# Output projection of a hybrid attention and HGRN2 layer: the order of its token tiles written out by hand, and its norms moved between ScalarE, VectorE and GpSimd

## The chip, the cores and the metric

The kernel runs on one core of one Trainium2 chip. The metric is the device time of one execution in microseconds (us). The core has a matrix engine (TensorE, PE in the rows), VectorE (DVE), ScalarE (ACT), GpSimd (POOL) and SyncE (SP), which in this kernel issues all the loads and stores. TensorE's weight loads are shown as PEld; they overlap its products.

## The reference

One layer over 2048 tokens of width 1024. A combined projection feeds two parallel groups of heads: differential attention (4 heads of width 128) and a bidirectional HGRN2 scan (4 heads of width 128). Each head's readout is normalised by its own root mean square, multiplied by a gate, and all 8 heads go through one output projection. The stage that changes computes this (lines cut to what matters):

```python
def _rms_norm(x, g):
    xf = x.astype(jnp.float32)
    return xf * lax.rsqrt(jnp.mean(xf * xf, axis=-1, keepdims=True) + EPS) * g.astype(jnp.float32)
def _merge(attn_o, ag, hgrn_o, hg, w_out):
    y = jnp.concatenate([attn_o * jax.nn.silu(ag), hgrn_o * jax.nn.silu(hg)], axis=-1)
    return y @ w_out
...
        y_lat = _merge(attn_lat, ag_l, hgrn_lat, hg_l, w_out[layer])
...
        x = _layer_norm(alpha * x + gate[:, None, :] * y_lat, ln_gain[layer], ln_bias[layer])
```

Everything is float32. The kernel writes each float32 factor of a product as a high part in a rounded form (F32R) and a remainder in the same form, so that one product becomes three: lo by hi, hi by lo, hi by hi.

## The kernel before, in words

The kernel has three stages: the projections with the scan beside them, the attention, and the output projection (class `Output`). The last one, from about 1820 us, is what changes. It works on 16 tiles of 128 tokens, t = 0 to 15. The weight of 1024 by 1024 stays in SBUF: its first 512 columns as `woh` and `wol`, the other 512 in slots that attention has left, so that they carry old names (`kh`, `kl`, `e`).

For each tile there is a **front** and a **back**.

- `front(t)` loads the gates `G` and the readouts `Od` of the tile (512 KB each). ScalarE squares the 8 heads in one instruction of 128x1024, VectorE sums each head's squares (TENSOR_REDUCE), ScalarE takes the root, VectorE its reciprocal `rs`, and GpSimd multiplies the readouts by it (L1269). TensorE turns the 8 heads (8 transposes of 128x128 into PSUM, two banks of four, `pt`). For each bank VectorE multiplies by the gate (L1278) and rounds to the high part (a cast, L1279), and GpSimd subtracts to get the low part (L1280). The two parts are the stationary operands of the tile's products.
- `back(t)` loads the tile's rows of `x`, runs 24 products for each half of the columns (8 row blocks by three products, 128x512 each, into a PSUM bank `py`), and after each half VectorE multiplies by `gate` (L1304), adds ALPHA times `x` (L1305) and takes statistics (L1307). Behind the second half comes the LayerNorm's end: VectorE aggregates, ScalarE takes a root, VectorE a reciprocal and the product `nb` (L1327), ScalarE applies both to the row block (L1328), VectorE multiplies by `lng` (L1329), GpSimd adds `lnb` (L1330), SyncE stores.

Even tiles keep their readouts and gated parts in slots named `kh` and `kl`, odd ones in slots named `e`; tiles 0 and 1 use `q` and `e` for `x` and `y` and their fronts and most products run inside attention. In `run` the programme writes for each tile the five first steps of the front two tiles ahead, then the back's first half, then what is left of the next tile's front. A scheduler orders the engines' queues in this stage, by its own estimate of times; it may put the loads much earlier, and it put the first loads of `x` for tiles 2 and 3 at about 1215 us. Inside attention the order of TensorE, ScalarE and VectorE is written by hand. Every engine, SyncE too, works through its own queue in order; an instruction that waits for another engine holds all that stand behind it.

The last tile has its columns cut in four parts of 256, and its end on VectorE in two halves.

Of the kernel before, what the change touches and what calls it, by code (L numbers as in the profile page):

```python
# [22 lines left out]
F32, F32R, U32 = dt.float32, dt.float32r, dt.uint32  # L23
AF = mybir.ActivationFunctionType
ALU = mybir.AluOpType
# [4 lines left out]
P = 128  # L30
D = 1024
KT = 8
# [3 lines left out]
NKT = KEYS // P  # L36
H = 4
BLK = 512
NBLK = SEQ // BLK
GRID_W = 64  # L40
ALPHA = 2.0 ** 0.25
EPS = 1e-5
LAMBDA_INIT = 0.2
UW = 256
# [74 lines left out]
class Build:  # L119
    def __init__(self, nc, tc, I, out):  # L120
        self.nc, self.tc, self.I, self.out = nc, tc, I, out
# [9 lines left out]
    def run(self):  # L131
        nc, tc = self.nc, self.tc
        pool = tc.tile_pool
        with pool(name="dram", bufs=1, space=DRAM) as self.dram, \
                pool(name="const", bufs=1) as self.const:
            self.dram_tiles()
            att, output = Attention(self), Output(self)
            with ExitStack() as keys, ExitStack() as proj, ExitStack() as out:
                held = self.phase_project(att, proj, keys)
                att.run(held, proj, keys, output, out)  # L140
                output.run(out)
# [670 lines left out]
NT = SEQ // P  # L812
# [16 lines left out]
class Attention:  # L829
# [18 lines left out]
    def open(self, keys):  # L848

        self.kv0 = self.b.pool(keys, "kv0", 1, side="right")  # L850
        self.kv1 = self.b.pool(keys, "kv1", 1, side="right")
# [272 lines left out]
class Output:  # L1124
    def __init__(self, b):
        self.b, self.nc = b, b.nc
        self.gated = {}

    def open(self, stack):
        self.wo = self.b.pool(stack, "wo", 1)  # L1130
# [88 lines left out]
    def run(self, out):  # L1219
        b = self.b  # L1220
        self.op = b.pool(out, "o", 2)
        self.xy = lambda t: [self.op.tile([P, D], F32, name=nm) for nm in "xy"]
        self.py = b.pool(out, "py", 4, space=PSUM)
        self.acc = lambda n: self.py.tile([P, BLK], F32, name="py")
        pt = b.pool(out, "pt3", 2, space=PSUM)
        self.bank = lambda: pt.tile([P, 4, P], F32, name="pt3")
        for nm in ("lng", "lnb"):
            self.broadcast(nm, b.I[nm].unsqueeze(0), out)
        for t in range(2):
            for _ in self.backs[t]:  # L1230
                pass
        for t in range(2, NT):
            for _ in range(5 if t + 2 < NT else 0):
                self.advance(t + 2)
            for n in self.back(t):
                if n == 1 and t + 1 < NT:
                    while self.advance(t + 1):
                        pass

    def advance(self, t):  # L1240

# [106 lines left out]
```

## Time and profile before

| | |
|---|---|
| median of three runs | 2031.61 us (2031.46 to 2032.01) |
| the profiled execution's own time | 2032.69 us |
| its span from the first to the last instruction | 2030.9 us, so 1.8 us lie around it |
| TensorE busy, whole span | 1913.6 us (94%) |
| VectorE, GpSimd, ScalarE busy | 71%, 47%, 45% |
| mean granted TensorE clock | 0.981 of full speed |

The chain that ended last is TensorE for 66% of the span and VectorE for 14%. In the output projection (about 1820 us to the end) each full tile takes TensorE some 12 us of work; the stretch is read by tiles below. A row of a timeline gives the start, the duration, the engine, the line, the operation with its operands and shapes and, in brackets, how long the engine had been idle and which engine's work ended that.

### The profile page before, as it was taken

The numbers are of one execution on the slowest core, as the hardware profiler recorded it, in microseconds if no ns is written. First come the engines' busy times: TensorE is split into PE (matmuls) and PEld (weight loads), VectorE is DVE, ScalarE is ACT, GpSimd is POOL, SyncE is SP. The second block draws the span as 40 slices with busy tenths as digits, with TensorE's granted clock in tenths as the row PEclk, the third lists the DMA queues.
The fourth block names the chain that finished last, engine by engine and source line by source line (L and its number), as shares of the span: only waits on it lengthen the run. The fifth ranks groups of instructions, "written<-read, shape, count | busy, mean of one in ns | idle before, by whom it ended". The sixth has DMA issues, their size and how long they took to land.

```text
span 2030.9 us, 32106 instructions
## 1 busy us (share of the span) xinstructions
PE 1913.6 (94%) x11716; PEld 1693.3 (83%) x11716; DVE 1438.3 (71%) x3022; ACT 920.4 (45%) x1383; POOL 955.6 (47%) x697
## 2 busy tenths in 40 slices
PE   5899999999989999999879999999999999998887
PEld 3689888998878898877667999999999999887676
DVE  8940475455676755678454279999999999967878
ACT  6731233222222222232100168999998889852211
POOL 6400063343554532535110047877877767755543
PEclk8999999999989999999889999999999999999999
DMA  5772564523344543353657652261261031145442
GB/s 221 248 221 81 186 220 164 182 99 125 113 136 150 167 151 138 110 169 102 199 169 229 199 148 59 68 169 54 62 169 57 28 102 37 51 136 173 154 139 92
DMA packets 177760, 278.05 MB, mean 137 GB/s; under 512 B 16577, under 2 KB 108993, under 8 KB 175554
## 3 DMA queue, kind: packets, MB, share of 16 engines
q1 hardware_dynamic: 177602, 276.00, 42.6%
q8 instruction: 93, 1.52, 0.3%
q14 instruction: 65, 0.53, 0.1%
HBM read 178.94 MB, written 97.00 MB: 136 GB/s over the span
## 4 chain that ended last, share of the span: by engine, by line
PE 66%; DVE 14%; DMA 10%; issue 4%; POOL 3%; ACT 2%; SPq 1%; DVEq 0%; POOLq 0%; ACTq 0%
PE pd L507 18%; PE po L1089 9%; PE pd L526 9%; PE s L1002 6%; PE s L1003 6%; PE pt L1069 6%; PE pl L723 4%; PE py L1301 2%; DVE wl L457 2%; DMA QLd<-e 1%; DMA KLd<-e 1%; PE pm L755 1%; DVE y L1305 1%; DVE wh L456 1%; DVE qq L731 1%
## 5 line engine op out<-in xcount | busy, mean ns | idle before, releaser
L1017 DVE TENSOR_SCALAR_CACHE_REDUCE e<-s 128x512 f32<-128x512 f32 (+1 forms) x512 | 372.8, 751 | 31.9 <-PE s L1003 31.5
L507 PE MATMUL pd<-hh,wl 128*128 128x512 f32 (+1 forms) x928 | 371.8, 401 | 0.0
L507 PE MATMUL pd<-hl,wh 128*128 128x512 f32 (+1 forms) x928 | 355.6, 383 | 0.0
L507 PE MATMUL pd<-hh,wh 128*128 128x512 f32 (+1 forms) x928 | 355.5, 383 | 0.0
L1052 POOL TENSOR_TENSOR e<-e,e 128x768 f32<-128x768 f32 (+1 forms) x192 | 351.5, 1860 | 2.6 <-ACT e L1045 0.2
L1026 ACT ACTIVATE e<-e,nm 128x2304 f32<-128x2304 f32 x128 | 286.5, 2238 | 1.7 <-DVE nm L1021 1.5
L728 POOL TENSOR_TENSOR kk<-kk,fb 128x512 f32<-128x512 f32 x126 | 170.5, 1353 | 169.7 <-DMA kk<-KD 136.5
L1002 PE MATMUL s<-kh,q 128*128 128x512 f32 (+1 forms) x640 | 244.3, 388 | 1.2 <-DVE w1l L1076 0.6
L1003 PE MATMUL s<-kl,q 128*128 128x512 f32 (+1 forms) x640 | 231.4, 371 | 0.0
L507 PEld LDWEIGHTS pd<-hh,wh 128*128 128x128 f32 x928 | 177.0, 191 | 34.3
L507 PEld LDWEIGHTS pd<-hh,wl 128*128 128x128 f32 x928 | 177.9, 192 | 27.6 <-DVE wl L457 0.5
L507 PEld LDWEIGHTS pd<-hl,wh 128*128 128x128 f32 x928 | 177.8, 192 | 27.1
L718 ACT COPY km<-kk 128x512 f32<-128x512 f32 x112 | 71.0, 635 | 271.6 <-POOL kk L728 179.9
L1047 POOL TENSOR_SCALAR e<-e,cf 128x1280 f32<-128x1280 f32 x64 | 86.2, 1346 | 175.3 <-DVE cf L1037 121.3
L1069 PE MATMUL pt<-eye,e 128*128 128x128 f32 x1152 | 162.8, 272 | 2.4 <-DVE rs L1268 0.9
L734 POOL TENSOR_TENSOR fb<-fb 128x512 f32<-128x512 f32 (+6 forms) x126 | 88.3, 701 | 162.4 <-DVE qq L731 152.3
L526 PE MATMUL pd<-wh,hl 128*128 128x256 f32 x512 | 150.8, 295 | 4.1 <-ACT wh L456 4.1
L723 PE MATMUL pl<-qq,km 128*128 128x128 f32 x896 | 131.3, 291 | 24.7 <-DVE qq L731 23.0
L723 PEld LDWEIGHTS pl<-qq,km 128*128 128x128 f32 x896 | 122.9, 197 | 37.1 <-issue 25.4
L1069 PEld LDWEIGHTS pt<-eye,e 128*128 128x128 f32 x1152 | 135.7, 140 | 21.2 <-issue 2.8
L526 PE MATMUL pd<-wl,hh 128*128 128x256 f32 x512 | 146.9, 287 | 0.1
L526 PE MATMUL pd<-wh,hh 128*128 128x256 f32 x512 | 146.7, 287 | 0.0
(286 smaller groups left out, 4463.7 us busy)
## 6 DMA issues: line engine op xcount, KB each, us to landing
wraw<-win SPq DMA_DIRECT2D x68, 512.0 KB
xst<-xT SPq DMA_DIRECT2D x24, 512.0 KB
fb<-FD SPq DMA_DIRECT2D x18, 512.0 KB
kk<-KD SPq DMA_DIRECT2D x18, 512.0 KB
kh<-KHd SPq DMA_DIRECT2D x16, 576.0 KB
FD<-e SPq DMA_DIRECT2D x32, 256.0 KB
KD<-e SPq DMA_DIRECT2D x32, 256.0 KB
Gd<-e SPq DMA_DIRECT2D x32, 256.0 KB
```

What stands on the lines that cost most here:

```text
L507: nc.tensor.matmul(ps[:, 0:n], a[:, k, cs], r[:, k, :], start=(k == 0 and j == 0), stop=(k == KT - 1 and j == 2))
L526: nc.tensor.matmul(ps[:, t, :], a[:, k, ts], r[:, k, :], start=(t == 0 and k == 0 and j == 0), stop=(t == 1 and k == KT - 1 and j == 2))
L723: nc.tensor.matmul(pl[:, e, ch, :], km[:, e, ch * P:ch * P + P], qm, start=True, stop=True)
L728: nc.gpsimd.tensor_tensor(out=o, in0=o, in1=total(fb, 1, 0, c), op=ALU.mult)
L734: nc.gpsimd.tensor_tensor(out=o, in0=o, in1=x, op=ALU.mult)
L1002: nc.tensor.matmul(ps[:, c:c + w], q[:, m, :], kh[m][:, a + c:a + c + w], start=True, stop=False)
L1003: nc.tensor.matmul(ps[:, c:c + w], q[:, 2 + m, :], kl[:, a + c:a + c + w], start=False, stop=True)
L1017: self.nc.vector.tensor_scalar(out=d[e][:, a:b], in0=d.pop(("s", m, i)), scalar1=1.0, scalar2=None, op0=ALU.mult, op1=ALU.max, accum_out=s ...
L1026: self.nc.scalar.activation(out=e, in_=e, func=AF.Exp, bias=self.tiles[t]["nm%d" % m], scale=1.0, accum_out=self.small(t, "z%d" % m))
L1052: self.nc.gpsimd.tensor_tensor(out=d["e0"][:, a:b], in0=d["e0"][:, a:b], in1=d["e1"][:, a:b], op=ALU.add)
L1069: self.nc.tensor.transpose(out=ps[:, k - a, :], in_=d["e0"][:, k * P:k * P + P], identity=self.b.eye)
L1089: nc.tensor.matmul(out, a[:, k - _GROUPS[g][0], :], w[:, :, k - _GROUPS[g][0], :], start=(op == self.value_ends[0] and k == k0 and j == 0) ...
```

## The change

The stage gets a written order for TensorE, ScalarE, VectorE and SyncE (GpSimd's queue is still the scheduler's). Tiles 0 and 1 are finished as before, then `tile(t)` runs for t = 2 to 15. Tiles 2 and 3 still have the old front. From tile 4 on:

- the readout norm is ScalarE's: 8 squares of 128x128 that also give each head's sum, a root, and after VectorE's reciprocal 8 scaled copies of 128x128 (`norms`, written half a tile after the loads landed and half a tile before the transposes);
- the next tile's transposes stand as two groups of four among the tile's first 24 products (`gates`), the high part is a copy on ScalarE, the low part a subtraction on VectorE (`rest`);
- the LayerNorm's end is two VectorE instructions of 128x1024 (L1369, L1373), with nothing left on GpSimd;
- a tile's second half leaves PSUM while the next tile's first products run (`steady`).

```diff
+            self.backs = {2: self.steady(2)}
+            self.fetch(4)
+            for t in range(2, NT):
+                self.tile(t)
...
+        products(half)
+        if before:
+            next(before)
+        if nxt:
+            self.gates(t + 1, 0)
+        products(2)
+        if nxt:
+            self.gates(t + 1, 1)
+        if before:
+            next(before, None)
+        if last:
+            return
+        products(2)
+        if nxt:
+            self.rest(t + 1)
+        next(back)
+        if t + 2 < NT:
+            self.norms(t + 2)
+        if t + 3 < NT:
+            self.fetch(t + 3)
+        products(KT)
...
+        for i in range(2 * H):
+            nc.scalar.activation(out=sq[:, i, :], in_=o[:, i, :], func=AF.Square, accum_out=ms[:, i:i + 1])
+        nc.scalar.activation(out=ms, in_=ms, func=AF.Sqrt, scale=1.0 / P, bias=self.b.eps)
+        nc.vector.reciprocal(out=rs, in_=ms)
+        for i in range(2 * H):
+            nc.scalar.activation(out=o[:, i, :], in_=o[:, i, :], func=AF.Copy, scale=rs[:, i:i + 1])
...
+        for j in range(4):
+            nc.tensor.transpose(out=ps[:, j, :], in_=o[:, i + j, :], identity=self.b.eye)
+        nc.vector.tensor_tensor(out=gt, in0=ps, in1=g[:, i:i + 4, :], op=ALU.mult)
+        nc.scalar.copy(out=self.gated[t][0][:, i:i + 4, :], in_=gt)
...
+        for i in range(0, KT, 4):
+            self.nc.vector.tensor_tensor(out=gl[:, i:i + 4, :], in0=self.late[t][1][:, 2 * H + i:2 * H + i + 4, :],
+                                         in1=gh[:, i:i + 4, :].bitcast(F32), op=ALU.subtract)
...
+        for ns in halves:
+            nc.vector.scalar_tensor_tensor(out=y[:, ns], in0=y[:, ns], scalar=mv[:, 0:1], in1=bc["lng"][:, ns],
+                                           op0=ALU.subtract, op1=ALU.mult)
+        nc.vector.reciprocal(out=rstd, in_=rstd)
+        for ns in halves:
+            nc.vector.scalar_tensor_tensor(out=y[:, ns], in0=y[:, ns], scalar=rstd, in1=bc["lnb"][:, ns],
+                                           op0=ALU.mult, op1=ALU.add)
+            b.store(dst[:, ns], y[:, ns])
```

**VectorE, one tile in the steady part.** This is a stretch of its queue before, from the end of a tile's first half on; `e_18992` are the next tile's readouts and then gated values, `e_19132` its high and low parts, `pt` the transposes' banks.

```order
L1304 TENSOR_TENSOR y<-py,gate 128x512
L1268 RECIPROCAL rs<-ms 128x8
L1305 SCALAR_TENSOR_TENSOR y<-x,y 128x512
L1278 TENSOR_TENSOR e_18992<-pt_19133,G 128x512
L1307 BN_STATS st<-y 128x6
L1279 CAST e_19132<-e_18992 128x512
L1278 TENSOR_TENSOR e_18992<-pt_19141,G 128x512
L1279 CAST e_19132<-e_18992 128x512
L1304 TENSOR_TENSOR y<-py,gate 128x512
L1305 SCALAR_TENSOR_TENSOR y<-x,y 128x512
L1307 BN_STATS st<-y 128x6
L1263 TENSOR_REDUCE ms<-e_19190 128x8
```

The same engine in the changed kernel, from the second half of one tile to the reciprocal for the tile two ahead:

```order
L1335 TENSOR_TENSOR y<-py,gate 128x512
L1336 SCALAR_TENSOR_TENSOR y<-x,y 128x512
L1338 BN_STATS st<-y 128x6
L1361 BN_AGGR mv<-st 128x2
L1312 TENSOR_TENSOR kh_19117<-pt_19278,G 128x512
L1312 TENSOR_TENSOR kh_19117<-pt_19291,G 128x512
L1369 SCALAR_TENSOR_TENSOR y<-y,mv,lng 128x1024
L1371 RECIPROCAL rstd<-rstd 128x1
L1373 SCALAR_TENSOR_TENSOR y<-y,rstd,lnb 128x1024
L1321 TENSOR_TENSOR kl_19277<-kh_19117,kl_19277 128x512 x2
```

The gate products and casts stood between the instructions of a tile's first half and its second; now the gate products stand behind the finished tile's second half and ahead of its LayerNorm's end. The casts and the sums of squares (TENSOR_REDUCE) are gone from the queue; the LayerNorm's end and the subtraction (L1321) have come in.

**GpSimd, the hand-over from attention.** `q_18067` and `e_18289` are the rows of tiles 0 and 1 at their LayerNorm's end, `e_18326` the readouts of tile 3. Before:

```order
L1269 TENSOR_TENSOR kh_18240<-kh_18240,rs 128x1024
L1280 TENSOR_TENSOR kl_18368<-kh_18240,kl_18368 128x512 x2
L1269 TENSOR_TENSOR e_18326<-e_18326,rs 128x1024
L1330 TENSOR_TENSOR q_18067<-q_18067,lnb 128x1024
L1330 TENSOR_TENSOR e_18289<-e_18289,lnb 128x1024
```

After:

```order
L1406 TENSOR_TENSOR kh_18240<-kh_18240,rs 128x1024
L1417 TENSOR_TENSOR kl_18368<-kh_18240,kl_18368 128x512 x2
L1467 TENSOR_TENSOR q_18067<-q_18067,lnb 128x1024
L1406 TENSOR_TENSOR e_18326<-e_18326,rs 128x1024
L1467 TENSOR_TENSOR e_18289<-e_18289,lnb 128x1024
L1417 TENSOR_TENSOR e_18518<-e_18326,e_18518 128x512 x2
```

Tile 3's multiplication by `rs` now stands behind the addition of `lnb` to tile 0's rows. On TensorE, tile 3's 8 transposes moved from behind tile 2's 24th product to behind its 12th.

**SyncE, the same place.** `lng`, `lnb` are the LayerNorm's gain and bias, `kh_18497` and in the changed kernel `kh_18499` are tile 4's readouts, the first `x` is tile 2's. Before:

```order
L125 DMA G<-Gd_73 128x8x128
L125 DMA lng<-lng 128x1024
L125 DMA lnb<-lnb 128x1024
L128 DMA Od_176<-oa 128x128
L128 DMA Od_177<-oa 128x128
L125 DMA kh_18497<-Od_166 128x1024
L128 DMA out<-q_18067 128x1024
L128 DMA out<-e_18289 128x1024
L125 DMA e_18596<-Od_167 128x1024
```

After:

```order
L125 DMA lng<-lng 128x1024
L125 DMA lnb<-lnb 128x1024
L128 DMA Od_176<-oa 128x128
L128 DMA Od_177<-oa 128x128
L128 DMA out<-q_18067 128x1024
L128 DMA out<-e_18289 128x1024
L125 DMA G<-Gd_73 128x8x128
L125 DMA kh_18499<-Od_166 128x1024
L125 DMA x<-xn 128x1024
```

Tile 4's gates and readouts and tile 2's rows of `x` are now issued behind the stores of tiles 0 and 1, and `lng` no longer stands behind tile 4's gates. The two loads of `x` at 1215 us are gone from there.

## Rows read from the trace of the kernel before

**Rows 1.** TensorE's own waits, 1820 to 2031 us: total, times, longest

```profile
PE py L1301 <- POOL e L1280: 14.6, 6, 5.5
PE py L1301 <- POOL kl L1280: 7.1, 5, 1.8
```

**Rows 2.** Chain that ended last, ahead of tile 8: start, duration, what

```profile
1909.61 1.83 DVE y L1305
...
1911.92 1.27 POOL kl L1280
```

**Rows 3.** Timeline of TensorE: first products of tiles 4, 14 and 15, transposes in tile 8

```profile
1859.25 0.40 PE L1301 MATMUL py<-woh,kl 128*128 128x512 f32 x1
...
1918.93 1.04 PE L1277 MATMUL pt<-eye,e 128*128 128x128 f32 x8
1919.72 0.48 PE L1301 MATMUL py<-kh,kl 128*128 128x512 f32 x1
...
1998.99 0.51 PE L1301 MATMUL py<-woh,kl 128*128 128x512 f32 x1 [0.22 <-POOL kl L1280]
...
2011.04 0.28 PE L1301 MATMUL py<-woh,e 128*128 128x256 f32 x1
```

**Rows 4.** Windows of tiles 8 and 13: span, engines busy, clock, DMA share, GB/s

```profile
1913.20:1927.10 13.90, 12.23 (x57) 9.81 (x57) 10.58 (x17) 3.15 (x5) 7.26 (x4) 1.00 0.58 190
...
1985.00:1999.00 14.00, 13.74 (x57) 10.94 (x57) 12.30 (x17) 1.73 (x3) 6.89 (x4) 0.88 0.35 114
```

**Rows 5.** Timeline of VectorE and GpSimd: alone and beside each other

```profile
1859.45 0.69 DVE L1304 TENSOR_TENSOR y<-py,gate 128x512 f32<-128x512 f32 x1 [2.42 <-PE py L1301]
1860.18 0.69 DVE L1305 SCALAR_TENSOR_TENSOR y<-x,y 128x512 f32<-128x512 f32 x1
...
1862.46 0.16 DVE L1327 SCALAR_TENSOR_TENSOR nb<-mv,rstd 128x1 f32<-128x1 f32 x1
1863.93 1.23 DVE L1329 TENSOR_TENSOR y<-y,lng 128x1024 f32<-128x1024 f32 x1 [1.31 <-ACT y L1328]
...
1903.96 1.90 POOL L1269 TENSOR_TENSOR e<-e,rs 128x1024 f32<-128x1024 f32 x1 [3.05 <-DVE rs L1268]
1904.06 1.81 DVE L1327 SCALAR_TENSOR_TENSOR nb<-mv,rstd 128x1 f32<-128x1 f32 x1
```

**Rows 6.** ScalarE by shape, whole run: busy us, mean ns, idle before

```profile
L1026 ACT ACTIVATION_READ_ACCUMULATOR e<-e,nm 128x1 f32 x128 | 26.1, 204 | 0.0
L1110 ACT ACTIVATE oa<-pt,rz 128x128 f32<-128x128 f32 x64 | 20.0, 369 | 4.3 <-PE pt L1106 4.3
L1150 ACT CAST G<-G 128x512 fp32r<-128x512 f32 x8 | 4.9, 610 | 0.0
L1312 ACT ACTIVATE rstd<-mv,eps 128x1 f32<-128x1 f32 x16 | 4.6, 290 | 82.3 <-DVE mv L1310 82.3
L1260 ACT ACTIVATE kh<-kh 128x256 f32<-128x256 f32 x4 | 1.7, 414 | 0.0
```

**Rows 7.** Timeline of the hand-over, all engines (SPq is SyncE issuing a DMA)

```profile
1825.61 0.61 SPq L125 DMA_DIRECT2D lng<-lng  x1
1827.84 0.48 PE L1301 MATMUL py<-woh,kl 128*128 128x512 f32 x1
1832.09 1.22 DVE L1329 TENSOR_TENSOR q<-q,lng 128x1024 f32<-128x1024 f32 x1 [1.95 <-DMA lng<-lng]
1833.57 2.39 POOL L1330 TENSOR_TENSOR q<-q,lnb 128x1024 f32<-128x1024 f32 x1 [1.40 <-DMA Od<-oa]
...
1841.00 0.34 SPq L128 DMA_DIRECT2D out<-e  x1
1841.43 0.38 SPq L125 DMA_DIRECT2D e<-Od  x1
...
1845.46 0.79 PE L1301 MATMUL py<-woh,e 128*128 128x512 f32 x1 [5.46 <-POOL e L1280]
...
1845.47 1.06 ACT L1260 ACTIVATE e<-e 128x1024 f32<-128x1024 f32 x1 [4.89 <-DMA e<-Od]
...
1849.63 0.39 PE L1301 MATMUL py<-wol,e 128*128 128x512 f32 x1
```

**Rows 8.** Windows of the hand-over: span, engines busy, clock, DMA share, GB/s

```profile
1828.00:1832.00 4.00, 4.00 (x19) 3.26 (x19) 2.08 (x4) 0.63 (x2) 1.72 (x1) 1.00 0.83 295
...
1844.00:1848.00 4.00, 2.54 (x6) 2.06 (x7) 3.90 (x7) 1.36 (x2) 3.07 (x2) 0.50 0.84 255
```

More of the change, by code (lines that the diff above doesn't have):

```diff
@@ L1127, in __init__ @@
         self.gated = {}
+        self.late = {}
     def open(self, stack):
@@ L1228, in run @@
             self.broadcast(nm, b.I[nm].unsqueeze(0), out)
-        for t in range(2):
-            for _ in self.backs[t]:
-                pass
[L1232 to L1238, printed above, removed]
+        nc = self.nc
+        with self.b.tc.manual_schedule(engines={nc.tensor.engine, nc.scalar.engine, nc.vector.engine, nc.sync.engine}):
+            for t in range(2):
+                for _ in self.backs[t]:
+                    pass
+            self.backs = {2: self.steady(2)}
+            self.fetch(4)
+            for t in range(2, NT):
+                self.tile(t)
+            for _ in self.backs[NT - 1]:
+                pass
@@ new lines, in tile @@
+    def tile(self, t):
+        back, before = self.backs[t], self.backs.get(t - 1)
+        nxt = t + 1 < NT
+        if nxt:
+            self.backs[t + 1] = self.steady(t + 1)
+        last = t == NT - 1
+        products = lambda n: [next(back) for _ in range(n)]
+        half = KT // 2 if not last else KT
+        products(half)
[11 more added lines that the diff above has]
+        products(2)
+        if nxt:
+            self.rest(t + 1)
[5 more added lines that the diff above has]
+        products(KT)
@@ new lines, in fetch, with norms @@
+    def fetch(self, t):
+        b = self.b
+        g = self.gp.tile([P, KT, P], F32, name="G")
+        b.load(g, b.Gd[t // 4][:, :, (t % 4) * P:(t % 4 + 1) * P])
+        pool, na, nb = self.slots[t % 2]
+        w = pool.tile([P, NKT, P], F32, name=na)
+        b.load(w[:, 0:2 * H, :].rearrange("p h v -> p (h v)"), b.Od[t])
+        self.late[t] = g, w
+    def norms(self, t):
+        nc, sm = self.nc, self.sm
+        o, sq = (self.late[t][1][:, i * 2 * H:(i + 1) * 2 * H, :] for i in range(2))
+        ms, rs = sm.tile([P, 2 * H], F32, name="ms"), sm.tile([P, 2 * H], F32, name="rs")
+        for i in range(2 * H):
[4 more added lines that the diff above has]
+            nc.scalar.activation(out=o[:, i, :], in_=o[:, i, :], func=AF.Copy, scale=rs[:, i:i + 1])
@@ new lines, in gates @@
+    def gates(self, t, half):
+        nc = self.nc
+        if t not in self.late:
+            while self.advance(t):
+                pass
+            return
+        g, w = self.late[t]
+        o, sq = (w[:, i * 2 * H:(i + 1) * 2 * H, :] for i in range(2))
+        if half == 0:
+            pool, na, nb = self.slots[t % 2]
+            gg = pool.tile([P, NKT, P], F32R, name=nb)
+            self.gated[t] = gg[:, 0:KT, :], gg[:, KT:2 * KT, :]
+        i = 4 * half
+        ps, gt = self.bank(), sq[:, i:i + 4, :]
+        for j in range(4):
+            nc.tensor.transpose(out=ps[:, j, :], in_=o[:, i + j, :], identity=self.b.eye)
+        nc.vector.tensor_tensor(out=gt, in0=ps, in1=g[:, i:i + 4, :], op=ALU.mult)
+        nc.scalar.copy(out=self.gated[t][0][:, i:i + 4, :], in_=gt)
@@ new lines, in rest, with steady, outside @@
+    def rest(self, t):
+        if t not in self.late:
+            return
+        gh, gl = self.gated[t]
+        for i in range(0, KT, 4):
+            self.nc.vector.tensor_tensor(out=gl[:, i:i + 4, :], in0=self.late[t][1][:, 2 * H + i:2 * H + i + 4, :],
+                                         in1=gh[:, i:i + 4, :].bitcast(F32), op=ALU.subtract)
+    def steady(self, t):
+        nc, b, sm, bc = self.nc, self.b, self.sm, self.bc
+        last = t == NT - 1
+        w = UW if last else BLK
+        x, y = self.xy(t)
+        b.load(x, b.I["xn"][t * P:t * P + P, :])
+        st = sm.tile([P, D // UW, 6], F32, name="st")
+        def outside(n):
+            ns = slice(n * w, n * w + w)
+            nc.vector.tensor_tensor(out=y[:, ns], in0=ps, in1=bc["gate"][:, ns], op=ALU.mult)
+            nc.vector.scalar_tensor_tensor(out=y[:, ns], in0=x[:, ns], scalar=ALPHA, in1=y[:, ns],
+                                           op0=ALU.mult, op1=ALU.add)
+            nc.vector.bn_stats(out=st[:, n, :], in_=y[:, ns])
+        for n in range(D // w):
+            ps = self.acc(3 - 2 * n)[:, 0:w]
+            half, off = divmod(n * w, BLK)
+            for k in range(KT):
+                gh, gl = self.gated[t]
+                wh, wl = self.w(half, k, slice(off, off + w))
+                for j, (a, r) in enumerate(((gl, wh), (gh, wl), (gh, wh))):
+                    nc.tensor.matmul(ps, a[:, k, :], r, start=(k == 0 and j == 0), stop=(k == KT - 1 and j == 2))
+                if not (n > 0 and k == KT - 1):
+                    yield
+                elif last and n < D // w - 1:
+                    yield
+            if n == 0 and not last:
+                outside(n)
+                yield
+            elif last and n < D // w - 1:
+                outside(n)
+        if not last:
+            yield
+        outside(n)
+        mv = sm.tile([P, 2], F32, name="mv")
+        nc.vector.bn_aggr(out=mv, in_=st[:, 0:D // w, :])
+        rstd = sm.tile([P, 1], F32, name="rstd")
+        nc.scalar.activation(out=rstd, in_=mv[:, 1:2], func=AF.Sqrt, bias=b.eps)
+        if not last:
+            yield
+        dst = b.out[t * P:t * P + P, :]
+        halves = [slice(n * BLK, n * BLK + BLK) for n in range(2)] if last else [slice(0, D)]
+        for ns in halves:
[4 more added lines that the diff above has]
+            nc.vector.scalar_tensor_tensor(out=y[:, ns], in0=y[:, ns], scalar=rstd, in1=bc["lnb"][:, ns],
+                                           op0=ALU.mult, op1=ALU.add)
+            b.store(dst[:, ns], y[:, ns])
```

## The prediction

> **What bounds the kernel now.** I read the busy table first: TensorE 94% of the span. That is a mean over three stages, so next TensorE's own waits in the stretch that changes. All of them, 21.7 us in 11 waits, are for one line, GpSimd's subtraction that makes the next tile's low part [rows 1]. The chain of waits ahead of tile 8 says why it is late: VectorE is held in its L1305 for 1.83 us, then come gate product and cast, then the subtraction of 1.27 us [rows 2]. The same L1305 takes 0.69 us where GpSimd is idle [rows 5].
>
> So the stage is bound in turn: TensorE works a tile off, then waits for VectorE and GpSimd, which stretch each other. The timeline of first products gives the tile's price: tile 4 begins at 1859.25 and tile 15 at 2011.04, 11 tiles in 151.8 us, **13.80 us each**. Tile 14, behind which no wait stands, takes 2011.04 - 1998.99 = **12.05 us** [rows 3]: that is TensorE's work with 8 transposes. The windows show a second loss: tile 8 keeps TensorE busy for 12.23 us at a granted clock of 1.00 (2.4 GHz), tile 13, after a longer wait, for 13.74 us at 0.88 [rows 4], some 1.5 us more.
>
> **The change part by part, tiles 4 to 14.** TensorE has the same 48 products and 8 transposes. A block of transposes costs its 0.79 us and makes the product behind it 0.48 instead of 0.39 us long [rows 3]; two blocks instead of one cost 0.09 us more. If nothing else waits, a tile takes 12.14 us. Gain: 11 x (13.80 - 12.14) = **18.2 us**.
>
> Does nothing else wait? I walk one tile, T being its first product's start.
>
> *VectorE* (GpSimd has no work left from here on, so I take the durations without it): the second half of the tile before, 0.73 us each from start to start for three instructions [rows 5], and its aggregate, from T + 0.4 to 2.8. The first gate product needs four transposes, which follow 12 products of 0.23 us: 3.5 to 4.2. The second needs 6 more products and 4 transposes: 5.4 to 6.1. The LayerNorm's end, two instructions of 128x1024 at 1.23 us as L1329 takes alone [rows 5], a reciprocal between them: to 8.8. Two subtractions, as L1305 alone: to 10.2. The tile's first half, which TensorE left at 6.6: to 12.4, and the reciprocal of tile t + 2: 12.6, which is T' + 0.4 of the next tile. Some 10.3 us of work in 12.14. Tile t + 1's low part is there at T + 10.2, **2 us ahead of its first product**. Below, this cover is gone if VectorE slips by 2 us in every tile.
>
> *ScalarE*: 0.3 us for the root, two copies of 0.61, 8 squares, a root, 8 scalings. A 128x128 instruction has a row at 369 ns, a 256-wide square one at 414, reading a sum 204 [rows 6]. Bounds for a square with its sum: 0.31 us (that row where two follow each other closely) to 0.62 (414 + 204); I take 0.42. From T + 6.8 squares to 10.2, root to 10.5; behind VectorE's reciprocal the scalings run from T' + 0.5 and four heads are ready at T' + 1.8, eight at 3.0; their transposes stand at T' + 2.8 and 4.7. Cover: 1 us for the first four. At the upper bound the squares end at 11.8 and the root at 12.1, still ahead of VectorE's reciprocal. So this part costs nothing.
>
> The Trainium skill, "ScalarE: Activation LUTs", section "Rules for kernel authors", speaks against this piece: it sends a multiplication to VectorE and budgets some 0.3 us per instruction plus 0.83 ns per element, so that one of 1024 columns costs far less than eight of 128. By that budget the 16 small instructions cost an estimated 6.5 us. The rows that I took give 5.9 (3.4 for the squares and 2.5 for the scalings).
>
> *Transfers*: tile t + 3's loads and tile t + 1's `x` go out behind the store, some 9 to 11 us into the tile; with 4 us to land (1841.43 to 1845.47, [rows 7]) they are there at T' + 3, wanted at T' + 6.8 and T' + 11. Covered by 4 us and more.
>
> **The hand-over, tiles 2 and 3.** Here the order loses. Before, tile 2's transposes for tile 3 stood behind 24 products and did not wait. Now they stand behind 12, at 1827.84 + 2.8 = 1830.6, and want tile 3's readouts multiplied by `rs` on GpSimd, behind the addition of `lnb` to tile 0, which waits for VectorE's product with `lng`, which waits for a load. That load landed at 1832.1 [rows 7], behind the gates of tile 4; without them it lands as early as 1829.7 (0.6 us of issue and 512 KB at the 295 GB/s of [rows 8]). I take 1831.0. Then: product 1.2, `lnb` 2.4, `rs` 1.9 us [rows 5, 7] and 0.3 between queues: transposes at 1836.8, done at 1837.7. TensorE idles 6.2 us. After its wait of 5.46 us before, the clock stood at 0.50, the 1.2 GHz level [rows 8], and ten products took 4.17 instead of 2.3 us (1845.46 to 1849.63, [rows 7]). I take the same 1.9 us here: tile 2's 36 remaining products end at 1848.0, when tile 3 begins (1845.5 before).
>
> The stores of tiles 0 and 1 now hold back tile 4's loads. Tile 1's LayerNorm runs behind GpSimd's `rs`: product to 1838.0, `lnb` to 1840.5, then store, gates, readouts, `x`. Before, store and readouts took from 1841.0 to 1845.4 [rows 7]; with 512 KB more at 295 GB/s the readouts land at 1846.7 and `x` at 1848.5. Squares, root, reciprocal and four scalings (3.4, 0.3, 0.2 and 1.3 us) end at 1852.0; the transposes stand at 1850.8 and wait 1.2 us. Tile 4 begins at 1848.0 + 12.15 + 1.2 = 1861.4, against 1859.25: **2.2 us lost**. Bounds: the clock holds, `lng` is early and the transposes do not wait: tile 4 at 1857.5; `lng` as late as before and the burst of six loads and a store lands 3 us later: 1865.5. I take the middle because each link has a row of its own.
>
> The last tile's end on VectorE is the same code, and TensorE's last product sets it both times. **Sum: 18.2 - 2.2 = 16.0 us.** The profiled execution's own time is 2032.69, which gives 2016.7; it lies 1.1 us above the median of the runs, so against 2031.61 the forecast is **2015.6 us**.
>
> **The rivals.**
>
> *The hand-over costs more.* The burst lands late or a second tile has to wait: tile 4 at 1865.5 to 1868, the steady gain stays. 2020 to 2022. For it: TensorE, VectorE, GpSimd and SyncE wait there in a ring, each in order. Against: readouts landed in 4 us beside a store. 15%.
>
> *The hand-over costs less* (the bound above): about 2012. 10%.
>
> *A tile stays above 12.14.* ScalarE's squares at 0.85 us or VectorE 1 to 2 us slower, and transposes or low parts come late: 12.6 to 12.8 a tile, 11 x 0.5 to 0.65 = 6 us lost, 2021.5. For it: the cover of four heads is only 1 us. Against: no row of ScalarE has such a price. 12%. The skill's rule on ScalarE is this rival's; by its budget it would not come.
>
> *VectorE becomes the bound, slower than before.* The rows that I took show VectorE with GpSimd idle. If its two-input instructions stay as slow as L1305 in [rows 2], the four of 512 columns cost 1.83 each, the two of 1024 some 2.4, the rest 4.7: 16.8 us a tile, 11 x 4.7 - 16 = 35 us slower, 2067. It decides from 13.6 us a tile on, where the 16 us are gone. Against: L1327, one column wide, takes 0.16 us alone and 1.81 beside GpSimd's L1269, ending with it [rows 5]; the changed tiles have no GpSimd. 3%. The Trainium skill, "SBUF — State Buffer", section "Who interferes with whom", says that a VectorE instruction with two SBUF inputs and a GpSimd instruction share a port which one holds to its end; by that rule the slow durations go with GpSimd, and the trace agrees (1.81 against 0.16).
>
> *The order does nothing measurable*, since each queue has a new wait that eats the gain: 2%.
>
> **How the numbers follow.** Forecast 58%, own range 2012.5 to 2019. The range for 8 in 10 takes in the better hand-over and most of the two dearer cases: 2010 to 2024. A measurement of this kernel tells some 0.2% (4 us) from no change: faster 94%, the same 2%, slower 4%.
>
> **What would show it.** Right: no wait of TensorE from tile 5 on, first products 12.1 us apart, granted clock 1.00, L1336 at 0.69 us, ScalarE's squares at 0.3 us with their sums, tile 4's first product near 1861. Wrong: TensorE waits on ScalarE's scaled heads in every tile, or on VectorE's subtraction; VectorE waits long for `x`; TensorE idles well over 6 us at tile 2.

## The result and the profile after

The changed kernel takes 2010.05 us (median of 4, 2009.12 to 2013.03) against 2031.53 us, a ratio of 0.990 (0.9883 to 0.9917): 21.5 us faster where 16 were forecast. That lies 0.05 us above the lower bound of the range of 8 in 10 and outside the forecast's own 2012.5 to 2019. Timed again beside the experiments it took 2007.23 against 2029.16 us, 0.9896 (0.9877 to 0.9915). The profiled execution took 2013.03 us with a span of 2011.2 us.

TensorE's own waits from 1820 us to the end (total, times, longest), which were 21.7 us in 11 [rows 1]:

```profile
PE pt L1414 <- POOL e L1406: 3.6, 1, 3.6
PE pt L1311 <- ACT kh L1293: 1.5, 1, 1.5
```

What is left lies at the hand-over; from tile 5 on nothing waits. The timeline of TensorE, with the first products of tiles 2, 3, 4 and 15:

```profile
1829.10 0.48 PE L1347 MATMUL py<-woh,kl 128*128 128x512 f32 x1
...
1844.88 0.40 PE L1347 MATMUL py<-woh,e 128*128 128x512 f32 x1
...
1860.68 0.40 PE L1347 MATMUL py<-woh,kl 128*128 128x512 f32 x1
...
1991.72 0.28 PE L1347 MATMUL py<-woh,e 128*128 128x256 f32 x1
```

Eleven tiles from 1860.68 to 1991.72 are 131.04 us, 11.91 each, where [rows 3] gave 13.80. The window of tile 8 (columns as in [rows 4]) shows TensorE busy for all of its time at the full clock, GpSimd with nothing:

```profile
1908.60:1920.80 12.20, 12.20 (x59) 10.05 (x58) 9.80 (x16) 6.94 (x30) 0.00 (x0) 1.00 0.53 178
```

The timeline of VectorE in that tile answers to [rows 2, 5]: the addition of `x`, L1336, took 1.83 us there as L1305 and takes 0.69 now, and the low part is done at 1918.07, 2.2 us ahead of tile 9's first product at 1920.24.

```profile
1909.25 0.69 DVE L1336 SCALAR_TENSOR_TENSOR y<-x,y 128x512 f32<-128x512 f32 x1
...
1914.19 1.28 DVE L1369 SCALAR_TENSOR_TENSOR y<-y,mv,lng 128x1024 f32<-128x1024 f32 x1
...
1916.78 1.29 DVE L1321 TENSOR_TENSOR e<-e,e 128x512 fp32r<-128x512 f32 x2
```

ScalarE's groups by shape from tile 4 on (busy, mean ns, idle before) show what its new work costs:

```profile
L1293 ACT ACTIVATE kh<-kh,rs 128x128 f32<-128x128 f32 x40 | 12.3, 389 | 13.2 <-DVE rs L1291 13.2
L1289 ACT ACTIVATE kh<-kh 128x128 f32<-128x128 f32 x40 | 11.8, 295 | 0.0
L1289 ACT ACTIVATION_READ_ACCUMULATOR kh<-kh 128x1 f32 x40 | 7.5, 186 | 0.0
```

### The profile page after: what moved, and what is told of

Same layout as the page of the kernel before. It is cut to its first block, busy times and chain, and to the rows that moved or that the text cites. A ratio compares the mean times of both kernels' runs of the same rounds, so it can differ in the third digit from the quotient of the medians.

```text
span 2011.2 us, 32263 instructions
## 1 busy us (share of the span) xinstructions
PE 1912.2 (95%) x11716; PEld 1693.7 (84%) x11716; DVE 1416.6 (70%) x3010; ACT 964.8 (48%) x1670; POOL 867.8 (43%) x648
## 4 chain that ended last, share of the span: by engine, by line
PE 72%; DMA 10%; DVE 9%; issue 3%; POOL 3%; ACT 2%; SPq 1%; DVEq 0%; POOLq 0%; ACTq 0%
PE pd L507 17%; PE po L1089 9%; PE pd L526 9%; PE py L1347 7%; PE s L1002 6%; PE s L1003 6%; PE pt L1069 6%; PE pl L723 4%; DMA QLd<-e 2%; DVE wl L457 1%; DMA KLd<-e 1%; PE pm L755 1%; PE s L1438 1%; DMA xst<-xT 1%; PE pt L526 1%
## 5 line engine op out<-in xcount | busy, mean ns | idle before, releaser
L718 ACT COPY km<-kk 128x512 f32<-128x512 f32 x112 | 71.0, 635 | 272.6 <-POOL kk L728 179.7
```

## The experiments

The runs differ by some us ahead of the stage that changes: tile 2's first product stands at 1827.84 in the profile of before, at 1829.10 and 1824.52 in two of the changed kernel. So besides the ratio (each against runs of the kernel before that were timed beside it) the table gives two lengths read from each profile: the mean distance of first products from tile 4 to tile 15, and the **stretch** from tile 2's first product to the end of the span. Each length is from one profile; the two of the changed kernel differ by 1.5 us in the stretch.

| kernel | ratio (interval) | us a tile | stretch, us |
|---|---|---|---|
| before | | 13.80 | 203.1 |
| the change, first profile | 0.990 (0.9883 to 0.9917) | 11.91 | 182.1 |
| after_again | 0.9896 (0.9877 to 0.9915) | 11.91 | 180.6 |
| order_only | 0.9972 (0.9957 to 0.9987) | 12.94 | 194.8 |
| order_end | 0.9944 (0.9926 to 0.9962) | 12.79 | 192.7 |
| engines_only | 0.9896 (0.9878 to 0.9914) | 11.94 | 179.7 |
| b_norm | 0.9997 (0.9984 to 1.0009) | 14.07 | 203.3 |
| b_end | 0.9952 (0.9935 to 0.9969) | 12.84 | 192.7 |
| b_lo | 1.0026 (1.0013 to 1.004) | 14.24 | 207.6 |
| b_end_norm | 0.9884 (0.9858 to 0.9909) | 11.97 | 180.3 |
| cover2 | 0.9929 (0.9908 to 0.9949) | 12.57 | 189.4 |
| hand3 | 0.9892 (0.9874 to 0.9909) | 11.91 | 179.3 |
| hand6 | 0.9879 (0.9862 to 0.9895) | 11.91 | 177.3 |
| hand7 | 0.9865 (0.9843 to 0.9887) | 11.91 | 175.7 |

### The order, or the engines?

**order_only** keeps the written order and gives the old engines their work back. The norm is split in its place: squares, sum and root stand ahead of the tile's first half, reciprocal and product behind it.

```diff
-            self.nc.vector.tensor_tensor(out=gl[...], ..., op=ALU.subtract)
+            self.nc.gpsimd.tensor_tensor(out=gl[...], ..., op=ALU.subtract)
...
+        nc.scalar.activation(out=sq, in_=o, func=AF.Square)
+        nc.vector.tensor_reduce(out=ms, in_=sq, op=ALU.add, axis=AX.X)
...
+        nc.gpsimd.tensor_tensor(out=o, in0=o, in1=rs.unsqueeze(2).broadcast_to([P, 2 * H, P]), op=ALU.mult)
...
+            nc.scalar.activation(out=y, in_=y, func=AF.Identity, bias=nb, scale=rstd)
+            nc.vector.tensor_tensor(out=y, in0=y, in1=bc["lng"], op=ALU.mult)
+            nc.gpsimd.tensor_tensor(out=y, in0=y, in1=bc["lnb"], op=ALU.add)
```

> The written order stays, but from tile 4 on the norm (wide square, sum on VectorE, product on GpSimd), the low part (GpSimd) and the LayerNorm's end (ScalarE, VectorE, GpSimd) go back to their old engines; only the high part's copy stays on ScalarE. Theory 'order': the transposes stand 2.8 us earlier, so the low part has 7 us instead of 4 and is there by T + 8; TensorE does not wait, tiles 11.9 us apart, 2009 to 2014 us, although L1336's kind of instruction takes 1.3 to 1.9 us again. Theory 'engines' (the gain comes from GpSimd having nothing left to do that slows VectorE): tiles 13 us and more, 2022 us or above.

**engines_only** is the kernel before with the new engines, ordered by its scheduler; the norm, the high and low part (tile 4 on) and the LayerNorm's end (tile 2 on) in the old `front` and `back`:

```diff
+            for i in range(NH):
+                nc.scalar.activation(out=sq[:, i, :], in_=o[:, i, :], func=AF.Square, accum_out=ms[:, i:i + 1])
...
+            for i in range(NH):
+                nc.scalar.activation(out=o[:, i, :], in_=o[:, i, :], func=AF.Copy, scale=rs[:, i:i + 1])
...
+            (nc.vector.tensor_copy if t < 4 else nc.scalar.copy)(out=gh[:, i:i + 4, :], in_=gt)
+            (nc.gpsimd if t < 4 else nc.vector).tensor_tensor(out=gl[:, i:i + 4, :], ...)
...
-        if last:
+        if t > 1:
...
+            halves = [slice(n * BLK, n * BLK + BLK) for n in range(2)] if last else [slice(0, D)]
```

> The kernel before, its scheduler's order, with the change's engines from tile 4 on: squares with sums and scaled copies on ScalarE, high part on ScalarE, low part on VectorE, LayerNorm's end as two VectorE instructions. Theory 'engines': nothing contends any more, low part there some 9.5 us into the tile; tiles of 11.9 to 12.3 us, 2010 to 2016 us. Theory 'order': the transposes still stand behind 24 products and the reciprocal of the norm behind the LayerNorm's end in VectorE's queue, so TensorE waits 0.6 to 2 us in most tiles: 12.5 to 13.5 us a tile, 2016 to 2028 us.

The theory "order", by which I had walked the tile, falls. The engines alone give a ratio of 0.9896, as all of the change does; the order alone gives a quarter of it (2024.72 us), 12.94 us a tile. The timeline of order_only, VectorE, GpSimd, TensorE, shows why:

```profile
1906.76 2.40 POOL L1373 TENSOR_TENSOR y<-y,lnb 128x1024 f32<-128x1024 f32 x1
1907.00 2.71 DVE L1337 SCALAR_TENSOR_TENSOR y<-x,y 128x512 f32<-128x512 f32 x1
...
1910.36 0.19 DVE L1293 RECIPROCAL rs<-ms 128x8 f32<-128x8 f32 x1
...
1910.62 1.90 POOL L1294 TENSOR_TENSOR e<-e,rs 128x1024 f32<-128x1024 f32 x1 [1.46 <-DVE rs L1293]
...
1912.58 0.66 PE L1312 MATMUL pt<-eye,e 128*128 128x128 f32 x4 [0.83 <-POOL e L1294]
```

L1337 has 0.69 us of work, begins beside GpSimd's `lnb` addition and takes 2.71: it ends 0.55 us behind that addition. Behind it stand the reciprocal, GpSimd's product and the transposes that TensorE waits for. **order_end** takes that addition away alone (order_only with the change's LayerNorm's end).

> The written order with the change's LayerNorm's end on VectorE, but from tile 4 on norm (wide square, sum on VectorE, product on GpSimd) and low part on GpSimd as before. It differs from the run with the order alone only in the LayerNorm's end. Theory 'lnb': in that run GpSimd's lnb addition held the first half's L1337 for 2.7 us, so that the reciprocal and the product with rs came 0.9 us late for the transposes in each tile; without it tiles are 11.9 to 12.1 us apart, 2006 to 2011 us. Rival 'any long GpSimd instruction': the product with rs (1.9 us) and the subtractions (1.3 us each) hold VectorE's instructions just as well; the waits stay at 0.5 us or more, 12.4 us a tile, 2013 us or above.

It brought 12.94 to 12.79 (2020.17 us), so the rival held. TensorE's waits in tiles 3 to 14, and the groups from tile 4 on (mean ns behind the busy time):

```profile
PE pt L1312 <- POOL kh L1294: 5.2, 6, 2.0
PE pt L1312 <- POOL e L1294: 4.1, 6, 0.7
```

```profile
L1337 DVE SCALAR_TENSOR_TENSOR y<-x,y 128x512 f32<-128x512 f32 x23 | 29.6, 1285 | 0.8
L1370 DVE SCALAR_TENSOR_TENSOR y<-y,mv,lng 128x1024 f32<-128x1024 f32 x12 | 24.5, 2044 | 0.0
...
L1322 POOL TENSOR_TENSOR kl<-kh,kl 128x512 fp32r<-128x512 f32 x10 | 17.7, 1789 | 14.8 <-ACT kl L1314 14.8
L1294 POOL TENSOR_TENSOR e<-e,rs 128x1024 f32<-128x1024 f32 x6 | 11.4, 1897 | 26.7 <-DVE rs L1293 26.7
```

The holding only moved: the written order puts GpSimd's subtractions beside L1370, which takes 2.04 us instead of 1.28, and they take 1.79 each instead of 1.29; L1337 is still held for each tile's second half (1.28 on the mean of both halves), by the product with `rs`. What the run doesn't separate is the length of the old norm itself: its sum stands in VectorE's queue (L1290, 1.21 us) and its product is one piece of 1.90 us, where ScalarE hands over its scaled heads one by one.

### One part at a time, in the old order

**b_norm**, **b_end** and **b_lo** are the kernel before with the new engines of the norm, of the LayerNorm's end or of the high and low part alone; **b_end_norm** has norm and end. In the diff of engines_only they are the first two pieces, the last, the third, and the first two with the last.

> The kernel before with one part of the change: from tile 4 on the readout norm is ScalarE's (eight squares with sums, eight scaled copies); low part and the lnb addition stay on GpSimd, the scheduler orders all. Theory 'held by GpSimd': a VectorE instruction that reads two tiles from SBUF waits for the end of the GpSimd instruction beside it (1.9 us for the product with rs, 2.4 for lnb). Without the product with rs and the sum of squares VectorE reaches the LayerNorm's end some 3 us earlier, lnb is over before the next L1305 begins, and TensorE stops waiting: 11.9 to 12.2 us a tile, 2007 to 2012 us. Rival 'all three parts are needed': low part and lnb still hold VectorE, 13 us a tile or more, 2018 us or above.

> The kernel before with one part of the change: the LayerNorm's end of tiles 2 to 14 as two VectorE instructions of 128x1024, nothing of it on GpSimd; norm and low part as before. Theory 'held by GpSimd': lnb (2.4 us) no longer holds L1305 for 1.9 us, which takes some 1.2 us out of the chain that TensorE waits for, while the product with rs still holds one instruction: about 12.4 us a tile, 2011 to 2017 us. Rival 'all three parts are needed': 13 us or more, 2018 us or above.

> The kernel before with one part of the change: from tile 4 on the low part is VectorE's and the high part a copy on ScalarE; the product with rs and the lnb addition stay on GpSimd. Theory 'held by GpSimd': the two long instructions of GpSimd stay and hold VectorE as before; the low part itself takes 0.7 us instead of 1.3 but stands behind more work in VectorE's queue: 13.4 to 13.9 us a tile, 2022 to 2030 us. Rival 'the low part is late because GpSimd makes it slowly': 12.5 us or less, 2018 us or below.

> The kernel before, its scheduler's order, with two parts of the change: LayerNorm's end on VectorE and norm on ScalarE; only the low part stays on GpSimd, the high part on VectorE. With the first of the two alone tiles took 11.9 to 15.5 us, with the second alone 12.3 to 18. Theory 'ring': each alone leaves one long GpSimd instruction that delays a store or a squares' sum, and with it loads and the squares that stand ahead of the LayerNorm's root in ScalarE's queue; with both gone TensorE's waits go: 11.9 to 12.2 us a tile, 2006 to 2012 us. Rival 'all three parts': the subtractions on GpSimd keep VectorE and TensorE waiting, 12.5 us or more, 2014 us or above.

Alone, the norm moves nothing that can be measured, the LayerNorm's end gives half, the low part makes it slower. Norm and end together give everything (2006.12 us). I had expected the norm alone to do it (2029.91 us for 2007 to 2012); the other two missed as well, b_end with 2022.23 us in its rival's range, b_lo with 2036.09 above both of its ranges. The norm's timeline, all engines, tile 6, shows a ring, in which late readouts make the LayerNorm's end late and with it the store that the next loads stand behind (the store at 1895.57, the next readouts' load at 1896.00):

```profile
1882.70 0.33 SPq L125 DMA_DIRECT2D kh<-Od  x1
...
1889.49 0.31 ACT L1261 ACTIVATE kh<-kh 128x128 f32<-128x128 f32 x1 [12.90 <-DMA kh<-Od]
1889.81 0.28 ACT L1321 ACTIVATE rstd<-mv,eps 128x1 f32<-128x1 f32 x1
...
1893.20 2.35 POOL L1339 TENSOR_TENSOR y<-y,lnb 128x1024 f32<-128x1024 f32 x1 [10.52 <-issue]
...
1893.76 2.33 DVE L1314 SCALAR_TENSOR_TENSOR y<-x,y 128x512 f32<-128x512 f32 x1
...
1899.16 0.80 PE L1310 MATMUL py<-woh,e 128*128 128x512 f32 x1 [5.93 <-POOL e L1289]
```

The readouts landed 6.8 us after their issue (4 us in [rows 7]). ScalarE's square, which needs them, stands ahead of the LayerNorm's root, whose input had been there since 1884.2. So tile 5's LayerNorm's end came 5.6 us late, and with it all that stands behind it in VectorE's queue. Its `lnb` addition then fell beside the first half's L1314 and cost another 1.6 us (2.33 for 0.69); TensorE waited 5.9 us for the next tile's low part. In b_end_norm the same queue is there, but the root comes at most 1.7 us late and TensorE waits for nothing from tile 4 on. That the long GpSimd instructions are what lets the delay grow in b_norm is argued from these rows; no edit shows it. The groups of b_end_norm from tile 4 on:

```profile
L1314 DVE SCALAR_TENSOR_TENSOR y<-x,y 128x512 f32<-128x512 f32 x22 | 15.1, 686 | 0.4
...
L1289 POOL TENSOR_TENSOR kl<-kh,kl 128x512 fp32r<-128x512 f32 x10 | 12.9, 1290 | 42.0 <-DVE kl L1288 42.0
```

Here GpSimd still subtracts, at its own 1.29 us. L1314 has its 0.69, because in this order none of VectorE's two-input instructions stands beside a subtraction; only each tile's second cast does, and takes 0.5 instead of 0.42 us.

### The cover

**cover2** adds work to VectorE in each tile's LayerNorm's end.

```diff
+        for _ in range(2 if 3 < t < NT - 1 else 0):
+            nc.vector.tensor_tensor(out=y, in0=y, in1=y, op=ALU.max)
         nc.vector.reciprocal(out=rstd, in_=rstd)
```

> The changed kernel with two more VectorE instructions of 128x1024 in the LayerNorm's end of tiles 4 to 14 (the larger of y and y, which leaves y as it is), some 1.25 us each, ahead of the subtractions. Theory 'cover of 2 us': the first low part is read 2.8 us after it is made and VectorE has 9.75 us of work in a tile of 11.91; 2.5 us more make VectorE the bound at 12.25 us and a little more, TensorE waits 0.3 to 0.7 us a tile for the subtraction or for the scaled heads; 4 to 8 us slower than the changed kernel: 2011 to 2016 us beside its 2007 to 2010. Rival 'no cover': TensorE waits for the whole 2.5 us in each tile, 27 us slower, 2034 us or above. Rival 'more cover than read from the rows': no change.

It took 2016.06 us, at the upper end of what was expected. From tile 6 on a tile takes 12.72 us. Of the 2.49 us that the pair takes, 0.81 come out and 1.68 were covered. What is late first is not the low part but the scaled heads. In tile 8, which begins at 1901.65, the reciprocal for them ends at 1904.17, and the four transposes, due 2.80 us into the tile (1904.45), begin at 1904.67 and take 1.21 instead of 0.60 us, each behind its head: 0.22 and 0.6 us.

```profile
1903.99 0.18 DVE L1291 RECIPROCAL rs<-ms 128x8 f32<-128x8 f32 x1
...
1904.67 1.21 PE L1311 MATMUL pt<-eye,e 128*128 128x128 f32 x4
```

### The hand-over

**after_again** is the changed kernel itself. **hand3** loosens the hand-over, **hand6** also takes GpSimd out of it, **hand7** moves one norm.

```diff
+            self.fetch(4)
+            self.early = {t: self.rows(t) for t in (2, 3)}
             for t in range(2):
                 for _ in self.backs[t]:
                     pass
...
-        (nc.vector if t == 1 else nc.gpsimd).tensor_tensor(out=o, ...)
+        (nc.vector if t in (1, 3) else nc.gpsimd).tensor_tensor(out=o, ...)
...
         products(2)
+        if t == 2:
+            self.gates(t + 1, 0)
```

hand6 adds the low part's line and the LayerNorm's end of tiles 0 and 1 here, hand7 the norm's line as well (and leaves it out of its old place):

```diff
+            self.norms(4)
...
-            nc.gpsimd.tensor_tensor(out=gl[:, i:i + 4, :], ...)
+            (nc.vector if t == 3 else nc.gpsimd).tensor_tensor(out=gl[:, i:i + 4, :], ...)
...
-        if last:
+        if last or t < 2:
```

> The changed kernel once more, unaltered, beside the others of this call. 2009 to 2013 us, a ratio of 0.988 to 0.992 to the kernel before. If what is lost at the hand-over (tile 2's transposes waiting 3.6 us, tile 3's 1.9 us with a lower clock behind it) belongs to the queues, both waits are there again at the same places; if it was chance of one execution, they differ by more than 1 us.

> The changed kernel with its hand-over loosened: tile 4's gates and readouts and the rows of x for tiles 2 and 3 are loaded ahead of the stores of tiles 0 and 1, tile 3's product with rs runs on VectorE instead of GpSimd, and tile 3's transposes stand behind tile 2's 24th product. Theory 'ring of queues' (the waits at tiles 2 and 3 come from GpSimd's lnb addition and from loads behind stores): both waits go, tile 4 begins 24 us behind tile 2 instead of 31.6; 7.5 us faster than the changed kernel, 2002 to 2005 us. Rival, 'transfers': the loads collide with the gain's and bias's and the attention's last stores, x and readouts land late all the same; 0 to 3 us faster, 2007 to 2011 us.

> The changed kernel with the hand-over loosened and taken off GpSimd as well: loads of x for tiles 2 and 3 and of tile 4's readouts ahead of the stores, tile 3's product with rs and its low part on VectorE, the LayerNorm's end of tiles 0 and 1 as two VectorE instructions, tile 3's transposes behind tile 2's 24th product. In the looser variant before, tile 3's low part waited 2.5 us, because GpSimd's lnb addition of tile 1 held VectorE's cast for 2.2 us. Theory 'held by GpSimd': that wait goes too, tile 2 takes some 13 us and tile 3 some 12, together 25 against 30.0 in the changed kernel and 28.7 in the looser variant: 2002 to 2004 us where the changed kernel has 2007. Rival: VectorE, which now has the work of both tiles' ends, is late with tile 3's gates and low part: 2 to 4 us of wait stay, 2005 to 2008 us.

> The hand-over without GpSimd once more, with tile 4's norm written ahead of tile 3's gates instead of behind them. In the run before, tile 4's scaled heads came 1.0 us late, because the reciprocal stood behind tile 2's first half in VectorE's queue, and ten products behind that wait ran at the lower clock: tile 3 took 13.7 us. Theory 'queue order': that wait and the lower clock behind it go, tile 3 takes 12.0 to 12.3 us, tile 2 stays near 13; 1.5 us faster than that run, 2001 to 2006 us. Rival: VectorE now waits for ScalarE's root ahead of tile 3's gates, tile 3's low part is late instead, and the tile keeps its 13 to 14 us.

The changed kernel's wait of 3.6 us at tile 3's transposes came back to the hundredth; that at tile 4's did not. The windows (columns as in [rows 4]) of the first and the second profile of the changed kernel, behind the same wait of 3.59 us, and TensorE's rows in the second:

```profile
1836.00:1840.00 4.00, 4.00 (x23) 3.38 (x22) 3.96 (x4) 0.00 (x0) 2.75 (x2) 1.00 0.00 0
...
1852.00:1856.00 4.00, 4.00 (x16) 3.25 (x15) 2.49 (x4) 2.18 (x11) 0.00 (x0) 0.69 0.00 0
```

```profile
1832.00:1836.00 4.00, 4.00 (x14) 3.19 (x13) 3.93 (x5) 0.00 (x0) 3.34 (x2) 0.59 0.14 56
1836.00:1840.00 4.00, 4.00 (x19) 3.31 (x18) 1.31 (x2) 0.00 (x0) 1.63 (x2) 1.00 1.01 312
```

```profile
1831.13 1.34 PE L1414 MATMUL pt<-eye,e 128*128 128x128 f32 x8 [3.59 <-POOL e L1406]
...
1844.86 1.21 PE L1311 MATMUL pt<-eye,kh 128*128 128x128 f32 x4
```

In the first the clock held behind that wait and fell behind the next one, in tile 3. In the second it fell soon behind the wait's end (0.50 from 1832 to 1835), and tile 3 then had no wait in the list, though its first four transposes took 1.21 us instead of 0.60 and the tile 12.69.

hand3 (2006.88 us, its ratio within the interval of the changed kernel) missed its 2002 to 2005. It lost its transposes' wait all but 0.5 us and got another, 2.5 us ahead of tile 3's first product. Its timeline:

```profile
1835.73 2.38 POOL L1474 TENSOR_TENSOR e<-e,lnb 128x1024 f32<-128x1024 f32 x1 [2.70 <-DVE e L1473]
...
1836.22 2.17 DVE L1423 CAST e<-e 128x512 fp32r<-128x512 f32 x1
...
1839.88 0.79 PE L1354 MATMUL py<-woh,e 128*128 128x512 f32 x1 [2.47 <-POOL e L1424]
```

The cast of 0.43 us begins beside tile 1's `lnb` addition and ends 0.28 us behind it. hand6 has no GpSimd there, the cast takes 0.43, tile 2 takes 13.05 us; but tile 3 waited 1.0 us for tile 4's heads and took 13.71, so that hand6 (2006.35 us) missed its 2002 to 2004. hand7 mends that: tile 2 13.26, tile 3 11.98 us, and one wait is left in the whole stage:

```profile
PE pt L1422 <- DVE e L1414: 0.8, 1, 0.8
```

Its stretch is some 5 us shorter than that of the changed kernel's second profile. By the times it is the fastest, 2004.56 us (2000.26 to 2007.27) at 0.9865 of before, but its interval reaches that of the changed kernel, so that the step beyond it is read from the stretch of one profile and not shown by the ratio.

## Why the prediction was right, point by point

**The bound.** That TensorE's work would set the tile is shown: 11.91 us a tile, no wait, clock 1.00. The step that was mis-sized is the price of a tile, 12.14. The 12.05 of tile 14 held a first product of 0.51 us, behind a wait, where an undisturbed one takes 0.40: engines_only, with the same one block of eight transposes and no wait, has 11.94. The 0.09 for a second block was not there: the change, with two blocks, has 11.91. The gain of the eleven tiles was 151.79 - 131.04 = 20.75 us instead of 18.2.

**Why the waits went.** The walk through a tile had the right order of events, and its durations without GpSimd held (L1336 0.69; VectorE busy for 9.8 us in the window above instead of 10.3). What it left open is which half of the change did it. It was the engines: engines_only and b_end_norm reach the same time without the written order, order_only and order_end do not with it. What the first two share with the change is that no two-input instruction of VectorE stands beside one of GpSimd from tile 4 on. That the holding is the cause, and not the shorter norm that comes with it, rests on the rows: the lost time appears in them as stretched instructions (2.71 for 0.69 us ahead of a wait of 0.83). No run keeps GpSimd busy beside the changed VectorE. The Trainium skill, "SBUF — State Buffer", section "Who interferes with whom", has VectorE instructions with two SBUF inputs wait for a GpSimd instruction that reads SBUF, and counts casts among those that can; the trace agrees (2.71 for 0.69, 2.17 for 0.43), while the gate product with one input in PSUM kept its 0.68 us beside GpSimd (L1278 in the kernel before).

**ScalarE.** Eight squares took 0.29 us each from start to start where I took 0.42, the scalings 2.46 us as forecast. The cover of the first four heads, 1 us by my walk, was 1.7 by cover2, and it is the first to go, ahead of the low part. The Trainium skill, "ScalarE: Activation LUTs", section "Rules for kernel authors", gave an estimate of 6.5 us for the sixteen; the trace has 4.8 (2.36 and 2.46), since short instructions one behind the other cost less than that budget.

**The hand-over.** Mis-sized by 2 us. From tile 2's first product to tile 4's I forecast 33.6 us (31.4 before); it took 31.6. The rows of the changed kernel, VectorE and TensorE:

```profile
1829.78 1.22 DVE L1466 TENSOR_TENSOR q<-q,lng 128x1024 f32<-128x1024 f32 x1
...
1835.71 1.09 PE L1414 MATMUL pt<-eye,e 128*128 128x128 f32 x8 [3.59 <-POOL e L1406]
...
1849.36 1.21 PE L1311 MATMUL pt<-eye,kh 128*128 128x128 f32 x4 [1.52 <-ACT kh L1293]
```

The gain `lng` was there for VectorE by 1829.8, 0.7 us behind tile 2's first product, not 3.2, so the transposes waited 3.6 us instead of 6.2. The wait for tile 4's heads was 1.5 us for the 1.2 forecast. The lower clock cost about the 2 us that I had put down, but by luck: I had it behind the wait in tile 2, and in this execution it came behind the one in tile 3. Tile 4's first product at 1860.68, near the 1861 that I gave as a sign, is luck as well: tile 2 began 1.3 us later than in the profile of before.

**The sum.** 20.75, less 0.2 at the hand-over, and 0.4 behind tile 15's first product (19.86 us to the end before, 19.48 after) make 21.0 us over the stretch, the stretch of the first profile as well (203.1 - 182.1), beside 21.5 by the medians. The profiled spans differ by 19.7 only, as tile 2 began 1.3 us later in that execution; in the second profile of the same kernel it began 4.6 us earlier, so the 1.3 can't be put down to the change. The 2012 that I gave to a better hand-over is near the result, but more of the 5 us beyond the forecast came from the tile's price (2.5) than from the hand-over (2.0).

**What stays open.** Which of hand3's three edits its shorter stretch needs; whether the written order is worth anything once the engines are changed; and why the same wait lowers the clock in one execution and not in the next. On the order, 11.91 against 11.94 and 11.97 us a tile is 0.3 to 0.7 us over the stage, below what the times can tell. At the hand-over it lost, by these profiles: from tile 2's first product to tile 4's engines_only takes 28.8 us and b_end_norm 29.1, the change 31.6 and 30.0.

## What to carry to other kernels

Ahead of an order, ask which instructions of two engines stretch each other: an instruction that takes longer beside GpSimd and always ends the same time behind its neighbour there is the mark, and moving the neighbour to an idle engine pays where moving the instruction only shifts the collision. Parts of such a change do not add up (0.0, 0.5 and -0.3% alone, 1.2% for two of them), so test pairs before dropping one that does nothing by itself. And look at what stands behind an instruction that waits for a load: here a LayerNorm's root waited 5.6 us for readouts that it does not use.

## What the runs showed of the hardware

A VectorE instruction that GpSimd holds ends a fixed time behind the end of the GpSimd instruction: 0.55 us for a two-input one of 128x512 (2.71 us beside 2.40 in order_only, and the same for L1305 in the kernel before), 0.28 for a cast (2.17 beside 2.38 in hand3), nothing for one column [rows 5]. A cast with one SBUF input is held just as two-input instructions are (2.17 us against 0.43), and GpSimd is held in turn: its subtraction took 1.79 us on the mean beside VectorE's two-input work, 1.29 without. A wait of TensorE of 3.59 us was followed by a granted clock of 1.00 in one execution and of 0.59 from 1832 to 1836 us, with the wait's end at 1831.13, in another of the same kernel (0.50 is the 1.2 GHz level).
